# One row block at a time in the first stage, both column halves of a token tile in turn in the last MLP chunk, and a rearranged list of delays

## The chip, the cores and the metric

The kernel runs on one core of a Trainium2 chip. The metric is the device time of one execution in microseconds (us). The engines are named as in the profile: PE is the matrix engine (PEld its weight loads), DVE the vector engine, ACT the scalar engine, POOL the GpSimd engine, SP the engine that issues nearly all DMA here.

## What is computed

One inference step of a two-layer backbone over 640 tokens (128 context and 512 latent) of width 1024. Per layer:

```python
h = x * (1 + sc_a) + sh_a                      # modulation from silu(c) @ w_ada + b_ada
mq, mk, mv, mo, mg, sq, sk, sv, nq, nk, nv = split(h @ w_in + b_in)
mix = concat(mlstm(mq, mk, mv, mo, mg), window_attention(sq, sk, sv), neighbourhood_attention(nq, nk, nv))
x = layer_norm(ALPHA * x + g_a * (mix @ w_out), ln1_g, ln1_b)
f = square(relu((x * (1 + sc_m) + sh_m) @ w_mlp1)) @ w_mlp2        # 1024 -> 4096 -> 1024
x = layer_norm(ALPHA * x + g_m * f, ln2_g, ln2_b)
```

## The kernel before

All products are fp32 carried by three products of split operands: every weight and activation is kept as a rounded high part and the rest, and `hi*hi + lo*hi + hi*lo` is summed in PSUM. `piece` (L366 on) loads 512 columns of a weight into one of four raw buffers (`wraw`), copies the high part on ACT (L371) and subtracts on DVE (L372) into one of eight split buffers (`wsp`).

Tokens are five tiles of 128. `gemm_feat` (product at L477, tile name gfeat) gives feature-major results in two halves of 320 tokens, 24 products for a block of 128 features and a half. `gemm_tok` (product at L393, tile gtok) gives token-major results, 512 columns for a tile, three products for each of K row blocks. PSUM tiles of both come from the pool `gp` with three buffers; `sp` (one buffer of two halves), `op` and `tp` serve the attention steps.

**Order.** PE's instructions stand in the order in which the program emits them; the other engines' order and the allocation of buffers are set by a list scheduler with the program order as priority, and SP's DMA issues with them. Attention, mLSTM, modulation and transposes (`to_feat`, named f0 to f4 after the first LayerNorm and g0 to g4 after the second) are generators in a queue. A planner keeps a planned time `self.T`; between products `pump` takes the steps whose due time has passed. The table `LATER` adds tenths of a microsecond to the due time of a named step (layer, name: {step: delay}).

**Start** (`start`, L292 on). The first modulation is computed in four parts q. Part q loads weights (adaw, 2 MB each) and the transposed inputs (xTv), runs 64 small products (L244), transposes them (L266) and then writes row blocks q and q+4 of the modulated input Xt (L328 to L330; the low part of q+4 on POOL). `first` is a `gemm_feat` of three blocks over row blocks in four groups (i, i+4), 36 products each. PE's order is part 0, part 1, group 0, part 2, group 1, part 3, groups 2 and 3. Its six weight pieces go through the four raw buffers.

**MLP** (`mlp`). The 32 blocks of the hidden layer go in five chunks. Chunk 0 has six blocks by `gemm_feat` (four in one call, then one each). Each block is copied from PSUM into a value tile of two buffers (ACT, L1454), squared with relu on DVE (L1356), rounded on ACT (L1357), and the rest is subtracted on POOL (L1358). After block 1 come the sums of the transformed activations (`t_sums`, four DVE operations of 1280 columns) and the splits 1 and 2 (`t_split`), after block 3 the first half of the LayerNorm's gain and bias on the residual (`ln_half`: two rows in raw buffers, ten DVE operations at L1268 and L1269), after block 5 the second half. Later chunks form their blocks in pairs with fewer products (gpair, L1348). Each chunk then runs `gemm_tok` over all five token tiles for the column half q = 0, then for q = 1; after it the evacuation `ev` adds to the residual (L1198 to L1203) and, in the last chunk, collects statistics (L1205). After q = 1 of the last chunk a tile is normalized (L1512 and L1254, L1255 in layer 1) and in layer 0 handed to `to_feat` for the next layer. Where `between` is given, `gemm_tok` runs all but two row blocks of the first tiles ahead; in chunk 0 it isn't given.

## Time and profile before

| | |
|---|---|
| median of 3 runs | 1726.15 us (1725.24 to 1726.2) |
| profiled execution | 1726.68 us, span 1724.8 us |
| PE busy | 1620.9 us, 94% |
| PEld busy | 1403.1 us, 81% |
| DVE busy | 1177.1 us, 68% |
| ACT busy | 716.8 us, 42% |
| mean granted clock of PE | 0.972 |
| chain that ended last | PE 75%, DVE 11%, ACT 5%, DMA 4%, issue 3% |

The span is the time from the first to the last instruction. The profile counts a matmul from its start to a modelled end, so neighbouring matmuls overlap; PEclk is the share of full clock that was granted (1.00 is 2.4 GHz, half of it 1.2 GHz). In a list of instructions a number in brackets is the time the engine sat idle before, and what ended it; x24 means that 24 instructions of the kind were merged into one row.

### The profile page before, as it was taken

What the parts mean: (1) busy time and instruction counts of PE and PEld (TensorE: products, weight loads), DVE (VectorE), ACT (ScalarE), POOL (GpSimd) and SP (SyncE); (2) the same over time, 40 slices, a digit from 0 to 9 for tenths busy, and PEclk for the clock granted to TensorE, in tenths of its full rate; (3) what the DMA queues carried; (4) which work ended last, traced back from release to release, by engine and by line L of the source; (5) the groups of instructions that cost most, each with busy time, mean ns of one, the idle gap of its engine ahead of it and who ended that gap; (6) DMA issues with size and microseconds to landing.
All of it is one profiled execution on the core that took longest, in us unless ns stands there. A gap on an engine that the chain in (4) does not pass through costs nothing.

```text
span 1724.8 us, 27638 instructions
## 1 busy us (share of the span) xinstructions
PE 1620.9 (94%) x10396; PEld 1403.1 (81%) x10396; DVE 1177.1 (68%) x2477; ACT 716.8 (42%) x1640; POOL 214.7 (12%) x204
## 2 busy tenths in 40 slices
PE   5999799999999999999999998999998999999996
PEld 3988687778968787879888886888788898898985
DVE  3368767659857575757685778675797667676768
ACT  2342466655414142424353424666464243332430
POOL 0151000000301010112200510000002021111210
PEclk9999899999999999999999997999999999999998
DMA  8554434332235454542324331222322132322222
GB/s 308 199 167 130 133 124 138 117 98 80 83 125 189 135 184 140 180 145 74 108 92 139 101 97 53 67 65 79 105 86 86 50 98 73 95 69 83 74 78 81
DMA packets 105857, 195.23 MB, mean 113 GB/s; under 512 B 16474, under 2 KB 43098, under 8 KB 100604
## 3 DMA queue, kind: packets, MB, share of 16 engines
q1 hardware_dynamic: 105724, 193.47, 35.0%
q8 instruction: 82, 1.34, 0.3%
q14 instruction: 51, 0.42, 0.1%
HBM read 185.16 MB, written 8.26 MB: 112 GB/s over the span
## 4 chain that ended last, share of the span: by engine, by line
PE 75%; DVE 11%; ACT 5%; DMA 4%; issue 3%; POOL 1%; SPq 1%; DVEq 0%; ACTq 0%; POOLq 0%
PE gtok L393 35%; PE gpair L1348 19%; PE gfeat L477 10%; PE adaps L244 2%; PE o L1058 2%; PE ptp L1042 2%; ACT P L1013 2%; PE s L999 1%; DVE nm L1006 1%; DVE wst L372 1%; DVE P L1020 1%; PE mli L819 1%; DMA adab<-in_b_ada 1%; DMA nbias<-in_nbias 1%; ACT PT L1050 1%
## 5 line engine op out<-in xcount | busy, mean ns | idle before, releaser
L393 PE MATMUL gtok<-wst,f1T 128*128 128x512 f32 x1920 | 461.0, 398 | 5.9 <-ACT f1T L1357 3.1
L393 PEld LDWEIGHTS gtok<-wst,f1T 128*128 128x128 f32 x1920 | 361.7, 190 | 97.3 <-issue 5.9
L477 PE MATMUL gfeat<-Xt,wst 128*128 128x320 f32 x1920 | 316.0, 320 | 11.9 <-ACT f L1454 4.9
L477 PEld LDWEIGHTS gfeat<-Xt,wst 128*128 128x128 f32 x1920 | 292.8, 194 | 23.9 <-ACT f L1454 6.0
L371 ACT CAST wst<-wrawt 128x512 fp32r<-128x512 f32 (+2 forms) x288 | 167.5, 599 | 277.4 <-PE gtok L393 214.4
L1358 POOL TENSOR_TENSOR f1T<-f,f1T 128x320 fp32r<-128x320 f32 (+1 forms) x116 | 130.3, 1125 | 932.3 <-ACT f1T L1357 822.2
L372 DVE TENSOR_TENSOR wst<-wrawt,wst 128x512 fp32r<-128x512 f32 (+2 forms) x288 | 197.9, 701 | 69.4 <-ACT wst L371 67.6
L1348 PE MATMUL gpair<-Xt,wst 128*128 128x320 f32 x1248 | 195.1, 309 | 0.0
L1348 PEld LDWEIGHTS gpair<-Xt,wst 128*128 128x128 f32 x1248 | 186.2, 188 | 6.2 <-issue 2.5
L1198 DVE TENSOR_TENSOR gtok<-gtok,row 128x512 f32<-128x512 f32 x110 | 76.7, 697 | 163.5 <-PE gtok L393 162.8
L1316 ACT CAST wst<-wrawt 128x512 fp32r<-128x512 f32 x156 | 94.5, 620 | 196.3 <-DVE gtok L1198 106.5
L1317 DVE TENSOR_TENSOR wst<-wrawt,wst 128x512 fp32r<-128x512 f32 x156 | 112.5, 733 | 34.2 <-ACT wst L1316 34.0
L393 PE MATMUL gtok<-wst,Xt 128*128 128x384 f32 (+1 forms) x720 | 125.1, 329 | 7.1 <-DVE wst L372 7.1
L393 PEld LDWEIGHTS gtok<-wst,Xt 128*128 128x128 f32 x720 | 115.6, 192 | 11.0 <-DVE wst L372 8.3
L393 PE MATMUL gtok<-wst,yT 128*128 128x512 f32 x480 | 117.9, 399 | 1.6 <-DVE wov L1198 1.6
L393 PEld LDWEIGHTS gtok<-wst,yT 128*128 128x128 f32 x480 | 88.2, 188 | 23.1 <-DVE wov L1198 2.4
L1348 PE MATMUL gpair<-tq,wst 128*128 128x320 f32 x624 | 100.9, 310 | 0.0
L1348 PEld LDWEIGHTS gpair<-tq,wst 128*128 128x128 f32 x624 | 93.8, 188 | 4.8 <-issue 4.2
L1013 ACT ACTIVATE P<-P,nm 128x512 f32<-128x512 f32 (+2 forms) x120 | 80.6, 673 | 32.8 <-DVE nm L1008 15.0
L1357 ACT CAST f1T<-f 128x320 fp32r<-128x320 f32 (+1 forms) x116 | 56.4, 488 | 76.1 <-DVE f L1356 75.5
L1356 DVE SCALAR_TENSOR_TENSOR f<-f 128x320 f32<-128x320 f32 (+1 forms) x116 | 68.6, 593 | 26.2 <-ACT f L1427 19.3
L1006 DVE TENSOR_REDUCE nm<-P 128x2 f32<-128x1024 f32 (+2 forms) x60 | 66.5, 1108 | 15.6 <-ACT P L1095 8.7
(245 smaller groups left out, 1910.7 us busy)
## 6 DMA issues: line engine op xcount, KB each, us to landing
wrawt<-in_w SPq DMA_DIRECT2D x256, 256.0 KB
adaw<-in_w_ada SPq DMA_DIRECT2D x40, 1024.0 KB
wrawt<-in_w_f SPq DMA_DIRECT2D x56, 256.0 KB
adaw<-in_w_ada SPq DMA_DIRECT2D x16, 512.0 KB
wrawt<-in_w_o SPq DMA_DIRECT2D x32, 256.0 KB
Dt<-md SPq DMA_DIRECT2D x40, 128.0 KB
nbias<-in_nbias SPq DMA_DIRECT2D x18, 256.0 KB
wrawt<-in_w_tb SPq DMA_DIRECT2D x16, 192.0 KB
```

Source lines behind the costliest of these rows:

```text
L371: nc.scalar.copy(ws[:, 0, :], raw)
L372: nc.vector.tensor_tensor(out=ws[:, 1, :], in0=raw, in1=ws[:, 0, :].bitcast(F32), op=ALU.subtract)
L393: nc.tensor.matmul(o, lhsT=A[YORDER[k] if A is self.Y else k][:, hl, t * 128 : (t + 1) * 128], rhs=ws[k][:, wl, :], start=(k == 0 and hl + ...
L477: nc.tensor.matmul(g[i, h], lhsT=w[i][k // 4][:, wl, (k % 4) * 128 : (k % 4 + 1) * 128], rhs=self.Xt[:, k, hl, h * 320 : (h + 1) * 320], s ...
L1006: nc.vector.tensor_reduce(out=nm[:, 0:2], in_=P[:, :, 0:nk], axis=AX.X, op=ALU.max, negate=True)
L1013: nc.scalar.activation(P[:, h, 0:nk], P[:, h, 0:nk], AF.Exp, bias=nm[:, h : h + 1], accum_out=nm[:, 2 + h : 3 + h])
L1198: nc.vector.tensor_tensor(out=v, in0=o, in1=gr, op=ALU.mult)
L1316: nc.scalar.copy(w[name][:, 0, :], src)
L1317: nc.vector.tensor_tensor(out=w[name][:, 1, :], in0=src, in1=w[name][:, 0, :].bitcast(F32), op=ALU.subtract)
L1348: nc.tensor.matmul(o, lhsT=w[:, wl, k * 128 : (k + 1) * 128], rhs=rhs(k, hl), start=(start and k + hl + wl == 0), stop=(k == 3 and wl == 1 ...
L1356: nc.vector.scalar_tensor_tensor(out=f, in0=f, scalar=0.0, in1=f, op0=ALU.max, op1=ALU.mult)
L1358: nc.gpsimd.tensor_tensor(out=y[:, 1], in0=f, in1=y[:, 0].bitcast(F32), op=ALU.subtract)
```

## The change

Three things. At the start, `first` goes over single row blocks (0, 4, 1, 5, 2, 6, 3, 7), 18 products each; PE's order becomes part 0, block 0, part 1, block 4, part 2, blocks 1 and 5, part 3, the rest; the third weight's two raw pieces lie in the pool `tmp`. In chunk 0 of the MLP one block of a call takes its two PSUM halves from `sp` (`spread`); split 2 follows block 2 and split 1 block 3, each in two halves; the first LayerNorm half comes after all six blocks, and the second half's two rows are kept in raw buffers while its operations run tile by tile in the evacuation of q = 0 (`ln_tile`); the first two token tiles run four row blocks ahead. In the last chunk `gemm_both` takes both column halves of a tile before the next tile; the second half's weights are put into buffers that are free by then (Xt in layer 1; `p`, `tmp` and `aw` buffers in layer 0). The last LayerNorm of layer 1 is done in halves for all tiles, as it was for the last one. `LATER` changes in most entries.

```diff
     "0f2": {0: 10},
-    "0fin4": {0: 28},
-    "0g4": {0: 55, 1: -10},
-    "0ga": {0: 5},
+    "0fin0": {0: -10},
+    "0fin2": {0: 5},
+    "0g0": {0: 12},
+    "0g3": {0: 42},
+    "0g4": {0: 148},
+    "0ga": {0: 4, 1: 4},
...
-    "0ml4": {1: 11},
+    "0ml4": {1: 167},
...
-    "0s03": {0: 38},
+    "0s03": {0: 119},
...
-    "1s03": {0: 52, 3: 30},
+    "1s03": {0: 83, 3: 30},
...
         for q in range(4):
+            for _ in range((0, 1, 1, 2)[q]):
+                next(first)
             if q == 0:
-                first = self.gemm_feat(*[I["w_f"][0, m] for m in ML_FIRST[0][0]], kgroups=[(i, i + 4) for i in range(4)])
+                first = self.gemm_feat(*[I["w_f"][0, m] for m in ML_FIRST[0][0]], kgroups=[(k,) for k in (0, 4, 1, 5, 2, 6, 3, 7)])
                 next(first)
                 load(1)
...
-            if q > 0:
-                next(first)
-            if q == 3:
-                nc.sync.dma_start(self.cst, I["cst"])
+        for _ in range(3):
+            next(first)
+        nc.sync.dma_start(self.cst, I["cst"])
...
+    def gemm_both(self, A, src, evac, between):
...
+        if self.l == L - 1:
+            place = [x[:, :, 0:512] for x in self.X]
+        else:
+            place = [self.pp.tile([128, 2, 512], F32R, tag="p", name="wst") for _ in range(4)]
+            place += [self.tmp.tile([128, 2, 512], F32R, tag="tmp", name="wst") for _ in range(2)]
+            aw = self.adp.tile([128, 2, 2, 512], F32R, tag="aw", name="wst")
+            place += [aw[:, 0], aw[:, 1]]
+        ws = [[self.piece(b, 512) for b in src[0]], None]
+        later = lambda: ws.__setitem__(1, [self.piece(b, 512, w) for b, w in zip(src[1], place)])
...
+        early = {}
+        for t in range(2):
+            early[t] = self.gp.tile([128, 512], F32, tag="g", name="gtok")
+            for k in range(K - 2):
+                mm(early[t], 0, t, k)
+                if k % 2 == 1:
+                    self.q(self.six(512))
+                if (t, k) == (0, 1):
+                    between()
+                    later()
+        for t in range(NT):
+            for q in range(2):
+                o = early[t] if q == 0 and t in early else self.gp.tile([128, 512], F32, tag="g", name="gtok")
+                for k in range(K - 2 if q == 0 and t in early else 0, K):
+                    mm(o, q, t, k)
...
+                evac[q](t, o)
+                self.pump()
...
-        w = [self.feat_pieces(src) for src in srcs]
+        w = [self.feat_pieces(src) for src in srcs[: 2 if len(kgroups) > 1 else None]]
+        if len(kgroups) > 1:
+            w.append(self.feat_pieces(srcs[2], lambda: self.tmp.tile([128, 512], F32, tag="tmp", name="wrawt")))
...
-                    if (i, h) not in g and i == 2 and len(kgroups) > 1:
+                    if (i, h) not in g and i == (2 if len(kgroups) > 1 else spread):
                         s = self.sp.tile([128, 2, 512], F32, tag="s", name="gfeat")
...
-            nc.scalar.copy(hi, self.t32[w])
-            nc.vector.tensor_tensor(out=lo, in0=self.t32[w], in1=hi.bitcast(F32), op=ALU.subtract)
+            for k in (slice(0, 2), slice(2, 4)):
+                nc.scalar.copy(hi[:, k], self.t32[w][:, k])
+                nc.vector.tensor_tensor(out=lo[:, k], in0=self.t32[w][:, k], in1=hi[:, k].bitcast(F32), op=ALU.subtract)
...
-                rest = (g for j in range(4, 6) for g in self.gemm_feat(I["w1"][l, j]))
-                for j, g in enumerate(itertools.chain(self.gemm_feat(*first), rest)):
+                rest = (g for j in range(4, 6) for g in self.gemm_feat(I["w1"][l, j], spread=4 - j))
+                for j, g in enumerate(itertools.chain(self.gemm_feat(*first, spread=1), rest)):
...
                     if j == 1:
                         self.t_sums()
-                        self.t_split(1, 2)
-                    if j in (3, 5):
-                        self.ln_half(l, 0, j // 2 - 1)
+                    elif j in (2, 3):
+                        self.t_split(4 - j)
+                self.ln_half(l, 0, 0)
+                lnr = self.ln_rows(l, 0, 1)
                 self.t_split(3, 4)
...
                     self.ln_add(r, q, o, gr[int(t == 0)][q], ALPHA if c == 0 else 1.0, st.get(t))
+                    if c == 0 and q == 0:
+                        self.ln_tile(t, 1, lnr)
...
-                    if last and t == NT - 1:
+                    if last:
                         for h in range(2):
...
-                        self.add(self.to_feat(r, t, A, B), "feat", f + (0.5 if t < 3 else 5.0), f"g{t}")
...
+                    self.add(self.to_feat(r, t, A, B), "feat", self.use("V", 2.5, f) + 0.5, f"g{t}")
...
+            if c == NC - 1:
+                self.gemm_both(ft, [[I["w2"][l, q, j] for j in blocks] for q in range(2)], [ev(q) for q in range(2)], left)
+                break
...
-                self.gemm_tok(ft, [I["w2"][l, q, j] for j in blocks], 512, ev(q), between=left if q == 0 else None, ahead=2 if c < 4 else 3, inter=gen if q else None)
+                self.gemm_tok(ft, [I["w2"][l, q, j] for j in blocks], 512, ev(q), between=(left or (lambda: None)) if q == 0 else None, inter=gen if q else None)
```

## Rows read from the trace of the kernel before

**Rows 1.** The page, part 1: busy us, share of the span, instructions.

```profile
PE 1620.9 (94%) x10396; PEld 1403.1 (81%) x10396; DVE 1177.1 (68%) x2477; ACT 716.8 (42%) x1640; POOL 214.7 (12%) x204
```

**Rows 2.** Busy time by stage: us, PE, PEld, DVE, ACT, POOL, clock, DMA.

```profile
18.68:30.26 11.58, 4.45 (x65) 2.51 (x66) 4.27 (x8) 2.32 (x5) 1.53 (x1) 1.00 0.83 288
...
124.00:375.00 251.00, 228.27 (x1833) 189.75 (x1832) 171.36 (x451) 130.21 (x343) 16.74 (x17) 0.95 0.39 124
...
441.18:488.04 46.86, 40.85 (x215) 37.16 (x218) 33.35 (x41) 17.72 (x30) 14.87 (x6) 0.85 0.30 90
488.04:905.26 417.22, 417.10 (x2319) 350.49 (x2318) 278.48 (x488) 147.32 (x299) 52.17 (x55) 1.00 0.42 139
905.26:923.73 18.47, 14.02 (x83) 13.46 (x83) 14.25 (x29) 8.15 (x20) 0.00 (x0) 0.82 0.57 180
...
1000.00:1225.00 225.00, 204.26 (x1623) 176.51 (x1622) 154.56 (x401) 124.13 (x328) 10.83 (x9) 0.93 0.24 73
...
1290.17:1340.22 50.05, 45.36 (x243) 41.25 (x244) 35.98 (x40) 19.31 (x32) 11.42 (x6) 0.90 0.24 76
...
1711.11:1724.80 13.69, 0.00 (x0) 0.00 (x0) 10.35 (x25) 0.00 (x0) 0.00 (x0) 0.60 0.29 115
```

**Rows 3.** Timeline, the start: start us, us, engine, line, operation [idle before].

```profile
19.00 0.93 SPq L369 DMA_DIRECT2D wrawt<-in_w_f  x2
...
26.13 1.08 PE L244 MATMUL adaps<-adaw,cs 128*32 128x128 f32 x16 [6.37 <-DMA adaw<-in_w_ada]
...
30.26 7.41 PE L477 MATMUL gfeat<-Xt,wst 128*128 128x320 f32 x36
...
34.43 1.57 POOL L330 TENSOR_TENSOR Xt<-xTv,Xt 128x640 fp32r<-128x640 f32 x1 [11.71 <-DVE xTv L329]
...
40.05 5.53 PE L477 MATMUL gfeat<-Xt,wst 128*128 128x320 f32 x36
```

**Rows 4.** Timeline, first MLP chunk of layer 0 (its PE rows with PE alone).

```profile
441.70 3.78 PE L477 MATMUL gfeat<-Xt,wst 128*128 128x320 f32 x24 [0.52 <-ACT f L1454]
448.32 24.07 PE L477 MATMUL gfeat<-Xt,wst 128*128 128x320 f32 x144 [2.85 <-ACT f L1454]
...
479.00 9.04 PE L393 MATMUL gtok<-wst,f1T 128*128 128x512 f32 x26 [1.35 <-POOL f1T L1358]
...
443.45 4.36 POOL L1358 TENSOR_TENSOR f1T<-f,f1T 128x640 fp32r<-128x640 f32 x1 [150.73 <-ACT f1T L1357]
...
451.45 1.78 POOL L1358 TENSOR_TENSOR f1T<-f,f1T 128x640 fp32r<-128x640 f32 x1 [3.64 <-ACT f1T L1357]
...
456.85 23.00 SPq L369 DMA_DIRECT2D wrawt<-in_w  x12
...
465.67 1.28 DVE L1269 TENSOR_TENSOR res<-res,lnrow 128x512 f32<-128x512 f32 x2
```

**Rows 5.** Timeline of PE, first MLP chunk of layer 1.

```profile
1295.86 3.78 PE L477 MATMUL gfeat<-Xt,wst 128*128 128x320 f32 x24 [0.52 <-ACT f L1454]
1300.70 21.38 PE L477 MATMUL gfeat<-Xt,wst 128*128 128x320 f32 x144 [1.06 <-ACT f L1454]
...
1329.18 11.04 PE L393 MATMUL gtok<-wst,f1T 128*128 128x512 f32 x35 [1.34 <-POOL f1T L1358]
```

**Rows 6.** Timeline of PE, seam between the layers.

```profile
888.05 5.79 PE L393 MATMUL gtok<-wst,f1T 128*128 128x512 f32 x24
...
907.29 1.06 PE L531 MATMUL pth<-ident,res 128*128 128x128 f32 x8 [2.03 <-DVE res L1512]
...
911.41 12.32 PE L477 MATMUL gfeat<-Xt,wst 128*128 128x320 f32 x71 [0.41 <-DVE Xt L539]
```

**Rows 7.** Timeline, last chunk and tail of layer 1.

```profile
1656.70 54.41 PE L393 MATMUL gtok<-wst,f1T 128*128 128x512 f32 x234
...
1712.14 0.69 DVE L1198 TENSOR_TENSOR gtok<-gtok,row 128x512 f32<-128x512 f32 x1
...
1717.70 1.22 DVE L1255 TENSOR_TENSOR res<-res,row 128x1024 f32<-128x1024 f32 x1
```

More of the change, by code (lines that the diff above doesn't have):

```diff
@@ L431, in gemm_tok @@
         if between is not None:
-            for t in range(ahead):
+            for t in range(2):
                 early[t] = self.gp.tile([128, 512], F32, tag="g", name="gtok")[:, 0:n]
@@ L452, in gemm_tok, with mm @@
             self.pump()
-    def feat_pieces(self, src):
-        return [self.piece(src[:, j * 512 : (j + 1) * 512], 512) for j in range(2)]
-    def gemm_feat(self, *srcs, kgroups=(range(8),)):
+    def gemm_both(self, A, src, evac, between):
         nc = self.nc
-        w = [self.feat_pieces(src) for src in srcs]
+        K = len(A)
+        if self.l == L - 1:
[7 more added lines that the diff above has]
+        later = lambda: ws.__setitem__(1, [self.piece(b, 512, w) for b, w in zip(src[1], place)])
+        def mm(o, q, t, k):
+            for hl, wl in ((0, 0), (1, 0), (0, 1)):
+                nc.tensor.matmul(
+                    o, lhsT=A[k][:, hl, t * 128 : (t + 1) * 128], rhs=ws[q][k][:, wl, :],
+                    start=(k == 0 and hl + wl == 0), stop=(k == K - 1 and wl == 1),
+                )
+        early = {}
+        for t in range(2):
+            early[t] = self.gp.tile([128, 512], F32, tag="g", name="gtok")
[11 more added lines that the diff above has]
+                    mm(o, q, t, k)
+                    if k % 2 == 1 and k < K - 1:
+                        self.q(self.six(512))
+                self.T += self.six(512)
+                evac[q](t, o)
+                self.pump()
@@ L461, in gemm_feat, with feat_pieces @@
+    def feat_pieces(self, src, raw=lambda: None):
+        return [self.piece(src[:, j * 512 : (j + 1) * 512], 512, raw=raw()) for j in range(2)]
+    def gemm_feat(self, *srcs, kgroups=(range(8),), spread=None):
+        nc = self.nc
+        w = [self.feat_pieces(src) for src in srcs[: 2 if len(kgroups) > 1 else None]]
+        if len(kgroups) > 1:
+            w.append(self.feat_pieces(srcs[2], lambda: self.tmp.tile([128, 512], F32, tag="tmp", name="wrawt")))
         g = {}
@@ L481, in gemm_feat @@
                             )
-                        if n % 2 == 1 and (ks is not kgroups[-1] or (h, n) != (1, len(ks) - 1)):
+                        if len(ks) == 1:
+                            self.T += self.six(160)
+                        elif n % 2 == 1 and (ks is not kgroups[-1] or (h, n) != (1, len(ks) - 1)):
                             self.q(self.six(320))
@@ L1250, in tail1, with ln_rows @@
             self.gemm_tok(self.Y, I["w_o"][l, q], 512, ev(q), by_block=q == 0)
-    def ln_out(self, r, lg, lb, dst):
-        nc = self.nc
-        nc.vector.tensor_tensor(out=r, in0=r, in1=lg, op=ALU.mult)
-        nc.vector.tensor_tensor(out=r, in0=r, in1=lb, op=ALU.add)
-        if dst is not None:
-            nc.sync.dma_start(dst, r)
-    def ln_half(self, l, i, h, dst=None):
-        nc, I = self.nc, self.I
-        hs = slice(h * 512, (h + 1) * 512)
+    def ln_half(self, l, i, h, dst=None):
+        row = self.ln_rows(l, i, h)
+        for t in range(NT):
+            self.ln_tile(t, h, row, dst)
+        self.use("V", 6.8)
+    def ln_rows(self, l, i, h):
         row = []
```

118 lines of the change are left out of this document (67 added, 51 removed).

## The prediction

> **What bounds the kernel now.** I read the head of the page first: TensorE is busy for 1620.9 of 1724.8 us [rows 1]. What is not matmul time is the only thing a reordering can win, so the next view is busy time and granted clock by stage, and in it only the stages where PE is not full or the clock is under 1.00 [rows 2]. The long middle, 488 to 905 us, has 0.12 us of idle PE in 417 us at clock 1.00 [rows 2]: whatever runs beside the matmuls there is free. The losses sit in five other places: the start, the first MLP chunk of each layer, the seam between the layers, the two attention stretches, and the tail. Two rates turn stages into losses: 144 products of 320 columns took 21.38 us, 148.5 ns each [rows 5], and 234 products of 512 columns took 54.41 us, 232.5 ns each [rows 7]; both at full clock. A stage's loss is its length less its products at these rates, so it holds the idle time and the time run at half clock after it. In the first chunk of layer 0 the clock reads 0.85 [rows 2], although idle is only 6 us of 47: a wait there costs about twice its length.
>
> **The start.** PE waits for weights of the modulation until 26.13, 6.37 us idle, and only after that runs the first 36 products, in 7.41 us where the next 36 took 5.53 [rows 3]. The change cuts each group of 36 into two of 18 and puts the first 18 ahead of the second modulation block. They need row block 0 only, which the first modulation block has produced, and the last two pieces of weights. These are issued as late as 19.00 [rows 3] because there are four raw buffers; the change gives them two of their own, and the modulation loads queued behind them on SP move up too. The stretch 18.68 to 30.26 has 11.58 - 4.45 = 7.1 us of idle PE [rows 2]; 18 products even at half clock (2 x 18 x 0.1485 = 5.3) fit in it. Gain if only they vanish from the path: 18 x 0.1485 = 2.7. If the loads behind also land so much earlier that no idle time is left: 7.1. If the 18 push the second modulation block later by 0.4: 2.3. The next late thing is row block 5, whose low half leaves POOL at 34.43 + 1.57 = 36.0 [rows 3]; it is needed behind two more steps of PE, so it stays hidden. I take **-3.5**, ends -7.1 and -2.3, nearer to the low end since the modulation loads stay bound by DMA, whose share in that stretch is already 0.83 [rows 2].
>
> **First MLP chunk, the six blocks.** In layer 0 the products stop 2.85 us at 448.32, for a copy that waits until POOL has released the first value tile; POOL's subtraction took 4.36 us there and 1.78 us the next time [rows 4]. From 441.70 - 0.52 = 441.18 to 448.32 + 24.07 = 472.39 PE did 7 x 24 products: 31.2 - 24.9 = 6.3 us lost. In layer 1, from 1295.86 - 0.52 = 1295.34 to 1300.70 + 21.38 = 1322.08 [rows 5]: 26.7 - 24.9 = 1.8. The change gives one block of each call two more PSUM halves, moves ten LayerNorm operations on DVE behind the blocks and halves the splits. The sixth group of products then needs no copy, but the seventh still waits for the first value tile: from 441.18 to 448.32 that took 7.1 us, with POOL at 1.78 instead of 4.36 it takes 4.6, and one group of 24 (3.6 us) covers it. So 1 us of wait stays, 2 if POOL is held up in part, and the clock may or may not hold. I take **-3.5** and **-1**; ends -6.3 and 0, -1.8 and 0.
>
> **First MLP chunk, the start of the second product.** From 472.39 to 479.00 + 9.04 = 488.04 PE did 15 + 1 + 26 = 42 products [rows 4]: 15.65 - 9.77 = 5.9 lost, waiting for the last block's POOL result. In layer 1, 1322.08 to 1340.22 with 51 products [rows 5]: 18.14 - 11.86 = 6.3. The change lets the second token tile's first four blocks go ahead: 12 products, 2.8 us more cover, which is as much as the wait itself. What is late next is weights. The rows of the second LayerNorm half now hold two of the four raw buffers through the whole pass, and the first half's hold the other two until its ten operations are done. Before, twelve pieces took 23.00 us to issue, 1.9 us each, and the LayerNorm half that ran beside them ended at 465.67 + 1.28 = 466.9 [rows 4]. Six pieces need 11.5 us; PE needs the last one 27 x 0.2325 = 6.3 us after it begins at about 468. They are on time if the LayerNorm half ends by about 462, and 5 us late if at 466.9. I take half, **-3** in each layer; ends -6 and 0. The LayerNorm operations that move into the evacuation cost nothing beside the matmuls: four operations of 0.69 are 2.8 us per tile, against 18 x 0.2325 = 4.2 us of products; without that cover they would cost 1.4 us a tile.
>
> **Seam between the layers.** Before, DVE has evacuation, statistics, normalization and the split of a tile inside 5.8 us of products [rows 6] and falls behind. The last gtok product ends at 888.05 + 5.79 = 893.84; the transposes of the last tile start at 907.29 after 2.03 us of waiting, and the products run again at full pace only from 911.41. From 905.26 to 923.73: 18.47 us for the transposes (1.06) and 72 products (10.7), 6.7 lost, clock 0.82 [rows 2]. With both halves of a tile in turn there are 11.2 us of products per tile, so the last tile finds DVE free: three operations of 0.69 [rows 7], statistics and normalization (an estimated 3 us) end some 5 us after the last product rather than 13. The 2.03 us wait goes. But the new delay list puts this tile's transposes 14.8 us late, so they still stand directly ahead of products that need their result, and the second wait (2 us) stays. **-3.5**, ends -6.7 and 0.
>
> **Tail.** 13.69 us with no product [rows 2]. The last tile's evacuation starts at 1712.14, 1.03 after the last product at 1711.11, and the previous tile's operations lie between its own: two of 1.22 [rows 7], one of them shown, and five shorter that I estimate at 0.9 to 1.2. With the tile order changed these are done before the last product ends: -1.03 - 2.44 - 0.9 = **-4.4**, ends -4.9 and -3. What follows the last operation, the output transfer, stays.
>
> **The new second half of the weights** of the last chunk is loaded while the first is used, into buffers that are otherwise dead by then. It is needed 42 x 0.2325 + 24 x 0.1485 = 13.3 us after the pass begins. Eight pieces at 1.9 us, the rate of [rows 4], would take 15.2: nothing, up to +2 in each layer.
>
> **The delay list.** It reorders side steps of the attention stretches on PE. Those stretches lose 22.7 us idle and 0.05 x 251 at half clock in layer 0, 20.7 and 0.07 x 225 in layer 1 [rows 2], some 72 us together. No row shows which steps change places; by the nearest ones a wait as at 448.32, with its half clock, is 6.3 us. I take 0, with ends of -8 and +8.
>
> **Sum.** -3.5 - 3.5 - 1 - 3 - 3 - 3.5 - 4.4 = -21.9. The profiled execution took 1726.7 us (span 1724.8 and 1.9 around it), 0.5 over the median of the runs, 1726.15. 1726.15 - 21.9 = **1704**. All good ends together give 1687 before the list, all bad ones 1721, or 1725 with the late second half.
>
> **Rivals.** *Raw buffers (A).* The LayerNorm rows keep the weights of the second product waiting: the two -3 go, and half of the -3.5 of layer 0 with the half clock that follows; the late second half costs 2. Then -22 + 6 + 1.7 + 2 = -12: 1714. For it: the transfers stood 23 us at this place already. Against: loads of the fifth and sixth block no longer stand behind LayerNorm rows.
> *POOL locked out (B).* POOL's 4.36 us came while DVE did subtractions and multiplications of two SBUF operands, its 1.78 us when DVE ran little beside it [rows 4]. The ten LayerNorm operations now come behind the six blocks, where PE waits for the last block's subtraction on POOL: 2.6 us more there in each layer eat the 2.8 us of new cover, and the two -3 go, but not the rest: 1726 - 16 = 1710.
> The Trainium skill (SBUF - State Buffer, Who interferes with whom) has the rule for it: a DVE instruction with two SBUF inputs and a GpSimd instruction that reads SBUF exclude each other for the whole instruction, and the first to issue wins. The 4.36 us agree with it; by that rule the move would not pay.
> *Slower (C).* The list puts one side step per attention block ahead of its data, in a PE queue that can't pass it; every product behind it waits and then runs at half clock, 6.3 us a time as at 448.32. Four such places beyond today's (25 us) decide it; six of them give 1704 + 38 = 1742. For it: 72 us are lost there already in this way. Against: most of the list's changes are under 1 us of planned time.
> *No change (D).* The gains are given back at the next wait on a chain that doesn't move. Against: nothing in these stages is tied to a fixed time, and PE is full from 488 to 905 [rows 2], so a shift is handed on. 1726.
>
> **How the numbers follow.** Forecast 0.57, A 0.18, B 0.10, C 0.10, D 0.05. The range: the forecast's own ends with the list's give 1690 to 1714, and A's late side reaches 1720; below 1690 and above 1720 (C, D) I leave about 0.2. So 1690 to 1720. A measurement of this kernel tells 0.2%, 3.5 us, from no change: faster holds forecast, A and B, 0.85; D 0.05; slower C, 0.10.
>
> **What would show it.** Right: 18 products of gfeat before 26 us; the wait at 448 under 2 us and the first-chunk stages above 0.95 clock; 27 products without a break at the start of gtok; the last tile's transposes not waiting for the normalization; under 10 us after the last product. Wrong: waits of PE on wst at the start of gtok (A), POOL over 3 us on the last block (B), the two attention stretches more than 10 us longer (C).

## The result, and the profile after

The changed kernel takes **1703.2 us** (median of 4 runs, 1699.7 to 1712.0) against 1726.2 beside it: a ratio of 0.987, 95% interval 0.983 to 0.991. The forecast was 1704, its range 1690 to 1720. The profiled execution has a span of 1699.4 us, 25.4 less than before, and TensorE is busy for 7.2 us less in it [rows 1]. First the head of the page, then busy time by stage, cut at the places that answer to those of [rows 2] (us, PE, PEld, DVE, ACT, POOL, clock, DMA share, GB/s):

```profile
PE 1613.7 (95%) x10396; PEld 1394.4 (82%) x10396; DVE 1188.2 (70%) x2489; ACT 715.3 (42%) x1648; POOL 213.8 (13%) x204
```

```profile
14.60:26.62 12.02, 8.04 (x84) 6.39 (x84) 6.72 (x16) 5.39 (x10) 2.47 (x1) 1.00 0.98 357
117.54:368.54 251.00, 233.90 (x1883) 192.60 (x1881) 176.46 (x460) 133.14 (x350) 17.44 (x17) 0.95 0.40 129
429.03:471.68 42.65, 38.48 (x218) 34.18 (x220) 40.25 (x50) 18.23 (x34) 15.46 (x6) 0.92 0.33 99
471.68:888.89 417.21, 417.08 (x2319) 350.71 (x2318) 284.42 (x496) 146.82 (x299) 51.89 (x55) 1.00 0.43 141
888.89:905.48 16.59, 13.53 (x81) 13.09 (x81) 8.86 (x20) 8.30 (x20) 0.00 (x0) 0.90 0.52 160
981.91:1206.91 225.00, 201.63 (x1635) 174.97 (x1636) 154.81 (x415) 123.64 (x329) 11.02 (x10) 0.95 0.25 75
1267.43:1316.28 48.85, 44.31 (x251) 39.38 (x250) 46.61 (x55) 24.14 (x47) 11.11 (x6) 0.93 0.26 81
1689.46:1699.40 9.94, 0.00 (x1) 0.00 (x0) 6.37 (x17) 0.00 (x0) 0.00 (x0) 0.68 0.14 53
```

The middle (471.68 to 888.89) is as full as before. To see where 25.4 us went, I cut the kernel at the first product of each kind in TensorE's timeline. Lengths in us, from one profiled execution each; "again" is a second profile of the changed kernel, from another session:

| stretch | before | after | again | after - before |
|---|---|---|---|---|
| start, to the first token projection | 58.60 | 52.14 | 53.25 | -6.5 |
| layer 0, projections and attention | 362.85 | 357.65 | 360.77 | -5.2 |
| layer 0, six blocks of the first chunk | 50.77 | 44.19 | 44.18 | -6.6 |
| layer 0, their second product | 49.54 | 51.38 | 51.54 | +1.8 |
| layer 0, the other chunks | 371.92 | 372.72 | 372.72 | +0.8 |
| seam, to layer 1's first token projection | 29.89 | 27.40 | 27.39 | -2.5 |
| layer 1, projections and attention | 346.69 | 347.41 | 349.23 | +0.7 |
| layer 1, six blocks | 51.66 | 46.44 | 46.46 | -5.2 |
| layer 1, their second product | 45.20 | 45.95 | 46.68 | +0.7 |
| layer 1, the other chunks | 343.99 | 344.18 | 344.15 | +0.2 |
| tail, after the last product | 13.69 | 9.94 | 9.93 | -3.8 |

The 0.8 us that layer 0's other chunks are longer go with one token tile's transposes: that stretch holds 2088 TensorE instructions where it held 2080, and eight transposes of a tile take 1.03 us.

The timelines behind the rows that moved. The start, TensorE and SP's queue (start, length, what; the gap before in brackets), to be held against [rows 3]:

```profile
9.51 5.49 SPq L389 DMA_DIRECT2D wrawt<-in_w_f  x6
...
17.58 0.90 PE L543 MATMUL gfeat<-Xt,wst 128*128 128x320 f32 x2 [2.98 <-ACT wst L392]
...
24.17 1.95 PE L262 MATMUL adaps<-adaw,cs 128*32 128x128 f32 x64
```

All six weight pieces are issued in one go, 18 products run in the stretch that was idle, and the second modulation block finds its weights there at 24.17, where it waited until 26.13 and was fed in pieces before.

The first chunk, layer 0 and then layer 1, against [rows 4, 5]:

```profile
420.45 33.68 PE L543 MATMUL gfeat<-Xt,wst 128*128 128x320 f32 x228
...
457.12 3.50 PE L414 MATMUL gtok<-wst,f1T 128*128 128x512 f32 x14 [0.24 <-DVE wst L393]
461.80 0.73 PE L414 MATMUL gtok<-wst,f1T 128*128 128x512 f32 x2 [1.18 <-POOL f1T L1428]
463.84 0.52 PE L414 MATMUL gtok<-wst,f1T 128*128 128x512 f32 x1 [1.31 <-ACT f1T L1427]
465.80 4.63 PE L414 MATMUL gtok<-wst,f1T 128*128 128x512 f32 x10 [1.44 <-POOL f1T L1428]
...
431.90 1.94 POOL L1428 TENSOR_TENSOR f1T<-f,f1T 128x640 fp32r<-128x640 f32 x1 [154.49 <-ACT f1T L1427]
...
455.50 6.25 POOL L1428 TENSOR_TENSOR f1T<-f,f1T 128x640 fp32r<-128x640 f32 x1 [6.61 <-ACT f1T L1427]
...
462.22 0.81 DVE L1426 SCALAR_TENSOR_TENSOR f<-f 128x640 f32<-128x640 f32 x1
...
1269.70 0.42 PE L543 MATMUL gfeat<-Xt,wst 128*128 128x320 f32 x1 [0.26 <-ACT Xt L606]
1270.97 28.52 PE L543 MATMUL gfeat<-Xt,wst 128*128 128x320 f32 x191 [0.86 <-DVE Xt L607]
...
1301.15 0.50 PE L414 MATMUL gtok<-wst,f1T 128*128 128x512 f32 x1 [0.48 <-DVE wst L393]
1302.61 0.73 PE L414 MATMUL gtok<-wst,f1T 128*128 128x512 f32 x2 [0.95 <-ACT wst L392]
1304.91 1.65 PE L414 MATMUL gtok<-wst,f1T 128*128 128x512 f32 x3 [1.57 <-DVE wst L393]
1306.98 18.26 PE L414 MATMUL gtok<-wst,f1T 128*128 128x512 f32 x70 [0.42 <-DVE wst L393]
```

In layer 0 the six blocks now run without a break; in layer 1 two short waits for the last token tile's Xt are left, 0.26 and 0.86 us. The second product starts worse than before. In layer 0 it waits 1.18 us for GpSimd's subtraction of the fifth block, which takes 6.25 us, and then 1.31 and 1.44 us for the sixth block, whose square comes only at 462.22, 8.2 us after the second product has begun. In layer 1 it waits for weights, 3.4 us in four waits. Before, layer 1's waits for Xt were longer, and 23 products behind the second took 5.17 us:

```profile
1287.96 0.41 PE L477 MATMUL gfeat<-Xt,wst 128*128 128x320 f32 x1 [1.14 <-ACT Xt L538]
1290.17 5.17 PE L477 MATMUL gfeat<-Xt,wst 128*128 128x320 f32 x23 [1.80 <-DVE Xt L539]
```

The seam, TensorE and then VectorE with the last tile's normalization (L1279 to L1585), against [rows 6]:

```profile
878.08 10.81 PE L543 MATMUL gfeat<-Xt,wst 128*128 128x320 f32 x72
889.31 1.07 PE L599 MATMUL pth<-ident,res 128*128 128x128 f32 x8 [0.43 <-DVE res L1585]
892.39 0.41 PE L543 MATMUL gfeat<-Xt,wst 128*128 128x320 f32 x1 [2.01 <-ACT Xt L606]
893.43 12.21 PE L543 MATMUL gfeat<-Xt,wst 128*128 128x320 f32 x71 [0.63 <-DVE Xt L607]
...
881.43 0.20 DVE L1279 BATCH_NORM_AGGREGATE bmv<-bst 128x2 f32<-128x12 f32 x1
881.54 0.77 DVE L1339 TENSOR_TENSOR res<-res,lnrow 128x512 f32<-128x512 f32 x1
...
888.37 0.80 DVE L1585 TENSOR_SCALAR res<-res,bmv 128x1024 f32<-128x1024 f32 x1
```

The tail, against [rows 7]: the last evacuation starts with nothing of the previous tile between its steps.

```profile
1683.74 5.72 PE L492 MATMUL gtok<-Xt,f1T 128*128 128x512 f32 x24
...
1689.50 0.70 DVE L1266 TENSOR_TENSOR gtok<-gtok,row 128x512 f32<-128x512 f32 x1 [2.31 <-PE gtok L492]
...
1694.84 1.41 DVE L1582 SCALAR_TENSOR_TENSOR res<-res,bmv,row 128x512 f32<-128x512 f32 x2
```

### The profile page after: what moved, and what is told of

Same layout as the page of the kernel before. It is cut to its first block, busy times and chain, and to the rows that moved or that the text cites. A ratio compares the mean times of both kernels' runs of the same rounds, so it can differ in the third digit from the quotient of the medians.

```text
span 1699.4 us, 27642 instructions
## 1 busy us (share of the span) xinstructions
PE 1613.7 (95%) x10396; PEld 1394.4 (82%) x10396; DVE 1188.2 (70%) x2489; ACT 715.3 (42%) x1648; POOL 213.8 (13%) x204
## 4 chain that ended last, share of the span: by engine, by line
PE 75%; DVE 11%; DMA 4%; issue 4%; ACT 4%; SPq 1%; POOL 1%; DVEq 0%; POOLq 0%; ACTq 0%
PE gtok L414 31%; PE gpair L1418 19%; PE gfeat L543 8%; PE gtok L492 6%; PE ptp L1110 2%; PE o L1126 2%; PE adaps L262 2%; PE s L1067 2%; ACT P L1081 1%; PE mli L887 1%; DMA adaw<-in_w_ada 1%; DVE res L1338 1%; DVE wst L393 1%; DMA nbias<-in_nbias 1%; DVE res L1339 1%
## 5 line engine op out<-in xcount | busy, mean ns | idle before, releaser
L414 PE MATMUL gtok<-wst,f1T 128*128 128x512 f32 x1440 | 349.4, 400 | 7.7 <-DVE wst L393 2.7
L414 PEld LDWEIGHTS gtok<-wst,f1T 128*128 128x128 f32 x1440 | 271.1, 190 | 80.4 <-issue 5.9
L543 PE MATMUL gfeat<-Xt,wst 128*128 128x320 f32 x1920 | 309.5, 317 | 10.2 <-ACT wst L392 4.9
L543 PEld LDWEIGHTS gfeat<-Xt,wst 128*128 128x128 f32 x1920 | 286.8, 191 | 22.5 <-ACT wst L392 6.1
L392 ACT CAST wst<-wrawt 128x512 fp32r<-128x512 f32 (+2 forms) x280 | 162.4, 597 | 224.7 <-PE gtok L414 157.4
L492 PE MATMUL gtok<-wst,f1T 128*128 128x512 f32 x360 | 85.5, 395 | 0.0
```

What stands on the lines that cost most here:

```text
L392: nc.scalar.copy(ws[:, 0, :], raw)
L414: nc.tensor.matmul(o, lhsT=A[YORDER[k] if A is self.Y else k][:, hl, t * 128 : (t + 1) * 128], rhs=ws[k][:, wl, :], start=(k == 0 and hl + ...
L492: nc.tensor.matmul(o, lhsT=A[k][:, hl, t * 128 : (t + 1) * 128], rhs=ws[q][k][:, wl, :], start=(k == 0 and hl + wl == 0), stop=(k == K - 1 ...
L543: nc.tensor.matmul(g[i, h], lhsT=w[i][k // 4][:, wl, (k % 4) * 128 : (k % 4 + 1) * 128], rhs=self.Xt[:, k, hl, h * 320 : (h + 1) * 320], s ...
```

## The experiments

All start from the changed kernel. Stretch lengths are cut as in the table above, each from the one profile of its run.

**The same kernel again.** No edit.

> The changed kernel once more, nothing edited. Its four runs lie between 1699.7 and 1712.0 us where the kernel before kept within 5 us. Theory 1: the spread sits in the stages whose waits the change left or made (the start of the second product in the first MLP chunk, 7.8 and 6.9 us lost in the profile at hand, and the attention stretches), so a second profile shows the start (to 52.3 us), the six blocks (33.7 us for 228 products) and the tail (9.9 us) within 0.3 us, and those stages different by several us. Theory 2: the whole is slower by a common factor, then the dense middle (chunks 1 to 3) is longer too. Time 1700 to 1712 by both.

1705.5 us (1702.7 to 1709.0), ratio 0.988 (0.986 to 0.990). The dense stretches repeat to 0.1 us; the start, the attention and layer 1's second product don't. So a small difference of a stage is read only in the stretches that repeat: eleven profiles with one and the same order in layer 0's attention have it at 357.4 to 362.9 us, and before, at 362.85, lies inside. The start, in the eleven profiles that have both of its edits, lies between 51.75 and 54.06.

**The start, in two halves.** In start_raw the third weight goes back into the four raw buffers:

```diff
-        w = [self.feat_pieces(src) for src in srcs[: 2 if len(kgroups) > 1 else None]]
-        if len(kgroups) > 1:
-            w.append(self.feat_pieces(srcs[2], lambda: self.tmp.tile([128, 512], F32, tag="tmp", name="wrawt")))
+        w = [self.feat_pieces(src) for src in srcs]
```

> Undoes one third of the change at the start: the third weight's two raw pieces go back into the four shared raw buffers, so the second modulation block's loads again stand in SP's queue behind a piece that waits for a free buffer; the order of the products stays one row block at a time. The first product of the first token projection starts at 58.60 us in the kernel before and at 52.14 in the changed one. Theory (both parts count, the queue 3.6 us and the 18 products in idle time 2.9 us): 55.0 to 56.5. If the whole gain is the queue: 58 to 59. If the whole gain is the product order: 52 to 53. The rest of the kernel is that of the changed one.

In start_grp the buffers stay and the order goes back:

```diff
-            for _ in range((0, 1, 1, 2)[q]):
-                next(first)
...
-                first = self.gemm_feat(*[I["w_f"][0, m] for m in ML_FIRST[0][0]], kgroups=[(k,) for k in (0, 4, 1, 5, 2, 6, 3, 7)])
+                first = self.gemm_feat(*[I["w_f"][0, m] for m in ML_FIRST[0][0]], kgroups=[(i, i + 4) for i in range(4)])
...
-        for _ in range(3):
-            next(first)
+            if q > 0:
+                next(first)
```

> The other half of the start: the third weight's raw pieces keep their own buffers, but the products are grouped in pairs of row blocks and taken after each modulation block, as in the kernel before. Theory (both parts count): first product of the first token projection at 54.5 to 56.0, the second modulation block's last TensorE product ends near 26 us as in the changed kernel instead of 29.7. If the whole gain is the queue: 52 to 53. If the whole gain is the product order: 58 to 59.

The first token projection starts at 54.90 in start_raw and 54.00 in start_grp, between 52.14 and 58.60 and a little earlier than I expected. By these profiles the order alone is worth 3.7 us, the free queue alone 4.6, both 6.5: each half alone brings more than half of the gain. What the second half adds to the first is not shown: 54.00 lies inside the 51.75 to 54.06 of the profiles with both edits, and 54.90 only 0.8 us outside. start_raw took 1703.9 us as a whole, in one run. Its timeline shows the piece that holds the queue at 18.71 and the modulation block behind it:

```profile
18.71 0.93 SPq L389 DMA_DIRECT2D wrawt<-in_w_f  x2
...
25.98 1.85 PE L262 MATMUL adaps<-adaw,cs 128*32 128x128 f32 x48
28.23 0.64 PE L262 MATMUL adaps<-adaw,cs 128*32 128x128 f32 x16 [0.40 <-DMA adaw<-in_w_ada]
```

start_grp as a whole took 1718.8 us in its one run, 13 to 16 above the changed kernel's two medians: layer 0's attention is 369.7 us long there, outside the 357.4 to 362.9 of the others, with one wait of 5.87 us where the longest in those is 3.2. My explanation, that the planner's clock moves with the grouping and the list of delays no longer fits, was not tested.

**Six blocks: the extra PSUM halves, or the LayerNorm's place?** no_spread takes the halves away:

```diff
-                rest = (g for j in range(4, 6) for g in self.gemm_feat(I["w1"][l, j], spread=4 - j))
-                for j, g in enumerate(itertools.chain(self.gemm_feat(*first, spread=1), rest)):
+                rest = (g for j in range(4, 6) for g in self.gemm_feat(I["w1"][l, j]))
+                for j, g in enumerate(itertools.chain(self.gemm_feat(*first), rest)):
```

> Undoes one part in the first MLP chunk alone: no block of the six gets the two extra PSUM halves; the layer-norm operations and the halved splits stay as in the changed kernel. The six blocks with what precedes them take 44.2 us in layer 0 and 46.4 in layer 1 in the changed kernel, without a wait of TensorE. Theory (the extra PSUM halves are what covers the copy of the first block): a wait for the copy comes back ahead of the sixth and seventh group of products, 47 to 51 us in layer 0 and 48 to 52 in layer 1. Rival (VectorE's order and the halved splits make the copy early enough): 44 to 45 and 46 to 47.

ln_old writes the first LayerNorm half, its two rows in raw buffers included, back among the blocks:

```diff
-                self.ln_half(l, 0, 0)
+                    if j == 3:
+                        self.ln_half(l, 0, 0)
                 lnr = self.ln_rows(l, 0, 1)
```

> The other part: the ten layer-norm operations of the first half are written back among the six blocks (behind the fourth), the extra PSUM halves stay. In the changed kernel's trace VectorE runs the first of these operations at 432.78, already between the squares of the first and second block, although they are written behind all six; so the place where they are written should matter little. Theory: 44.0 to 45.0 us and 46.0 to 47.0 us for the six blocks, as in the changed kernel, and the second product's start within 2 us of its 51.4 and 46.0 to 46.7. Rival (moving them behind the blocks is what freed GpSimd): the first block's subtraction takes over 3 us instead of 1.94, and the stretch is 2 to 4 us longer.

In no_spread the six blocks take 45.78 us in layer 0 and 48.12 in layer 1, 1.6 and 1.7 more than with the halves: in layer 0 between my theory and the rival, in layer 1 at the low end of the theory. Two waits of 0.5 to 0.65 us for the copy came back in each layer; in layer 0:

```profile
432.44 3.78 PE L543 MATMUL gfeat<-Xt,wst 128*128 128x320 f32 x24 [0.52 <-ACT f L1524]
436.76 21.39 PE L543 MATMUL gfeat<-Xt,wst 128*128 128x320 f32 x144 [0.55 <-ACT f L1524]
```

The second product takes 50.31 and 46.48 us behind them, so of blocks and product together 0.5 us is left in layer 0 and 2.2 in layer 1. The one run took 1705.6 us, like the changed kernel.

In ln_old the six blocks take 46.56 and 49.30, 2.4 and 2.8 more. My theory (the written place matters little) falls. In layer 0 the rival holds: GpSimd's first subtraction takes 6.37 us while VectorE runs LayerNorm beside it, and the copy behind it keeps TensorE waiting. In layer 1 it is VectorE's own order: the last tile's split into Xt stands behind LayerNorm operations, and TensorE waits 2.41 us for it instead of 0.86.

```profile
438.35 6.37 POOL L1428 TENSOR_TENSOR f1T<-f,f1T 128x640 fp32r<-128x640 f32 x1 [156.18 <-ACT f1T L1427]
...
445.22 17.86 PE L543 MATMUL gfeat<-Xt,wst 128*128 128x320 f32 x120 [2.12 <-ACT f L1524]
...
1283.33 29.81 PE L543 MATMUL gfeat<-Xt,wst 128*128 128x320 f32 x191 [2.41 <-DVE Xt L607]
```

But the second product then starts better: 49.54 and 40.71 us instead of 51.4 and 46.0. Blocks and product together are 96.10 and 90.01 with the old place, 95.57 and 92.39 with the new one. So moving the LayerNorm half behind the blocks mostly moved the loss: the sum gained 0.5 us in layer 0 and lost 2.4 in layer 1. The one run of ln_old took 1709.6 us, with layer 1's attention at 351.3, the longest of all profiles; its total says nothing of this edit.

**Second product: weights or GpSimd?** rows_late issues the LayerNorm's rows behind the six weight pieces, so that no row holds a raw buffer ahead of a weight; the ten operations that need the first two rows move with them:

```diff
-                self.ln_half(l, 0, 0)
-                lnr = self.ln_rows(l, 0, 1)
+                self.use("V", 6.8)
+                lnr = []
...
+                def left():
+                    self.ln_half(l, 0, 0, busy=False)
+                    lnr.extend(self.ln_rows(l, 0, 1))
```

> In the first MLP chunk the LayerNorm rows of both halves and the ten operations of the first half are put behind the six weight pieces of the second product, so the pieces take the raw buffers first; the order of PE and the planned times stay. Theory A (raw buffers held by the rows keep the weights waiting): the waits of PE on wst at the start of the second product (0.2 us in layer 0, 3.4 us in layer 1) vanish, the loss of that stage falls from 6.9 to under 3 us in layer 1. Theory B (LayerNorm operations on DVE shut POOL out): the subtraction of block 4 in layer 0, 6.25 us, falls to under 3, and the 3.9 us of waits on the last blocks' results fall below 2; the loss there falls from 7.8 to about 3. By both together the time falls by 6 to 9 us, 1694 to 1697; by A alone by 4, by B alone by 4. Rival: the ten operations now delay the first evacuation, the products stop for a PSUM buffer instead, and the time stays at 1703.

1709.1 us (1704.9 to 1711.1), no gain. TensorE's waits for weights are gone in both layers. In layer 0 the stretch is 49.4 us, 2.0 shorter; in layer 1 it is 49.0, 2.3 to 3.1 longer: now the last block is late there too.

```profile
1312.21 0.50 PE L414 MATMUL gtok<-wst,f1T 128*128 128x512 f32 x1 [2.09 <-ACT f1T L1428]
1318.26 12.06 PE L414 MATMUL gtok<-wst,f1T 128*128 128x512 f32 x43 [5.56 <-POOL f1T L1429]
...
1312.23 5.98 POOL L1429 TENSOR_TENSOR f1T<-f,f1T 128x640 fp32r<-128x640 f32 x1 [6.60 <-ACT f1T L1428]
```

In layer 0 the fifth block's subtraction is back at 1.80 us, yet the sixth block stays late, for a reason that I had not listed: ScalarE's copy of its second half out of PSUM stands in ScalarE's queue behind a weight cast that waits 4.56 us for a transfer.

```profile
464.46 0.62 ACT L392 CAST wst<-wrawt 128x512 fp32r<-128x512 f32 x1 [4.56 <-DMA wrawt<-in_w]
464.98 0.42 ACT L1525 COPY f<-gfeat 128x320 f32<-128x320 f32 x1
```

That copy starts 6.2 us after the second product has begun, and in layer 0 of the changed kernel just as late (6.2); in ln_after and ln_pool below it starts 0.2 us after. So late weights also reach TensorE through ScalarE's copy, without a wait of TensorE for weights. No run takes this apart.

So several causes stand one behind the other, and taking one away hands the stall to the next. ln_after, on top of seam_early (below), takes away all of them: rows in other buffers, the LayerNorm operations behind the sixth block, its subtraction on VectorE.

```diff
+                def left():
+                    for h in range(2):
+                        row = self.tmp.tile([128, 2, 512], F32, tag="tmp", name="lnrow")
...
+                    done = self.relu2(ft[j], f.rearrange("p h t -> p (h t)"), sub=nc.vector if j == 5 else None)
...
+                    if c == 0 and q == 0:
+                        with self.tc.issue_after(done.ins):
+                            self.ln_tile(t, 0, lnr[0])
```

> seam_early, and in the first MLP chunk of both layers: the layer-norm rows go into the two buffers that the sums of the activations leave (no raw weight buffer is held), all twenty layer-norm operations are queued on VectorE behind the sixth block's last step, and that step, the sixth block's subtraction, goes on VectorE instead of GpSimd. Reading of the runs so far: at the start of the second product TensorE waits for the raw buffers (weights, layer 1), for GpSimd's subtraction held up beside VectorE's layer-norm operations (both layers), and for the square of the last block, which stands behind layer-norm operations on VectorE. All three go here. The stretch from the first product with the squares to the first pair product takes 51.4 us (layer 0) and 46.0 to 46.7 (layer 1) in the changed kernel; theory: 44.5 to 48 and 40 to 43, the whole kernel 6 to 11 us below seam_early, 1688 to 1694. Rival (the layer-norm operations, now between the evacuations, make the second column half's weights late): the same stretches 50 to 53 and 45 to 48 with a wait on the weights at the start of the second half, the total within 3 us of seam_early's 1699.3.

ln_pool is ln_after with the sixth block's subtraction on GpSimd again, and the LayerNorm queued behind that block's square:

> ln_after with the sixth block's subtraction left on GpSimd; the twenty layer-norm operations stand on VectorE directly behind the sixth block's square, so they run while GpSimd subtracts. If operations on VectorE that read two inputs from SBUF hold up GpSimd, the sixth block's subtraction takes 5 to 6.5 us instead of 1.8, TensorE waits 3 to 5 us for it in each layer, and the kernel is 5 to 10 us slower than ln_after. If only the order on VectorE counts (the square behind the layer norm), it takes 1.8 to 2.1 us and the kernel is within 3 us of ln_after.

ln_after takes **1685.4 us** (1683.0 to 1691.3), ratio 0.976 (0.974 to 0.979); ln_pool 1686.8 (1680.3 to 1689.0), the same ratio; both are better than I expected of ln_after. The second product is 43.6 and 44.6 us in layer 0 and 39.0 in layer 1 for both, 7 to 8 us less than in seam_early and dense in layer 1:

```profile
1296.46 39.19 PE L414 MATMUL gtok<-wst,f1T 128*128 128x512 f32 x168
```

GpSimd's subtraction took 1.79 and 1.81 us in ln_pool, although LayerNorm operations run from its start on; here it was a VectorE operation beside it that took 2.06 instead of 0.68 us.

```profile
461.42 1.79 POOL L1429 TENSOR_TENSOR f1T<-f,f1T 128x640 fp32r<-128x640 f32 x1 [5.09 <-ACT f1T L1428]
...
460.49 1.29 DVE L1339 TENSOR_TENSOR res<-res,lnrow 128x512 f32<-128x512 f32 x2
461.69 2.06 DVE L1340 TENSOR_TENSOR res<-res,lnrow 128x512 f32<-128x512 f32 x1
```

So the first of the two expectations for ln_pool falls and the second holds: the engine of that subtraction is not what costs the 7 us. What does is the order on VectorE or the held buffers, with ScalarE's copy behind them; both runs change these together, and their shares are not shown.

**The seam.** seam_early puts the last LayerNorm's operations behind layer 1's first token projection and lets the last tile's transposes go early; seam_ln does the first alone (it keeps the delay of 148):

```diff
-                self.ln_half(l - 1, 2, m // 2, self.xd)
+                self.use("V", 6.8)
...
+            for h in range(2):
+                self.ln_half(l - 1, 2, h, self.xd, busy=False)
...
-    "0g4": {0: 148},
+    "0g4": {0: 10},
```

> Gain and bias of the last LayerNorm of layer 0 on the residual (twenty DVE operations of 0.68 us) are put behind the next layer's first token-major projection, and the delay of the last tile's transposes is 1.0 us instead of 14.8. Theory: at the seam those operations stand between the short operations of the last tile's reciprocal root (881.4 to 889.2 us for what takes 3 us in the tail), and the transposes stand directly ahead of products that need them; without both, the normalization ends by 884, the transposes run inside the 72 products, the waits of 0.43, 2.01 and 0.63 us and the half clock behind them go: 4 to 5 us, 1698 to 1699. Rival 1: the transposes now come too early and PE waits for the normalization, 1 to 3 us: 1701 to 1704. Rival 2: the moved operations hold up the next stage (gates, output-gate buffer), and the gain is lost there: 1703.

> One of the two edits of seam_early alone: the twenty layer-norm operations of layer 0's last norm are put behind the first token projection of layer 1, and the last token tile's transposes stay where the changed kernel's delay list puts them (delay 148). Theory (both the interleaved operations and the place of the transposes count): the stage at the layer seam takes 24 to 26 us (27.4 in the changed kernel, 22.1 in seam_early); the last tile's chain of ten short operations on VectorE takes some 3 us instead of 7.7. If the operations on VectorE explain it all: 22 to 23. If the place explains it all: 27 to 27.6.

seam_early: 1699.3 us (1694.4 to 1706.7), ratio 0.985 (0.983 to 0.988), seam 22.07 us instead of 27.4; the range of its runs overlaps that of the changed kernel, so the gain is read from the seam. seam_ln: a seam of 26.48, just above what I expected, 1705.7 us in one run. The last tile's chain on VectorE, ten short operations and the normalization, is 3.6 us long in it instead of 7.7 (881.43 to 889.17 above), yet this is worth only 0.9 us; the place of the transposes is worth 4.4 with it. With the transposes behind 42 products instead of 72, their result is there when it is needed:

```profile
877.86 6.41 PE L543 MATMUL gfeat<-Xt,wst 128*128 128x320 f32 x42
884.11 1.04 PE L599 MATMUL pth<-ident,res 128*128 128x128 f32 x8
884.90 15.20 PE L543 MATMUL gfeat<-Xt,wst 128*128 128x320 f32 x102
```

**Both halves of a tile in turn.** no_both takes the last chunk in two passes again (`if c == NC - 1` becomes `if c == NC`):

> Undoes the last chunk's part alone: its second product goes in two passes over the five token tiles, one for each column half, as in the kernel before; everything else is the changed kernel. Theory: the time from the last TensorE product to the end goes back from 9.94 us to 13.5 to 14.0, and the stretch from the last pair products of layer 0 to the first weight product of layer 1 loses the little that it had gained (27.4 us to 28.5 to 31); the whole kernel 5 to 7 us above the changed one (about 1711, with a spread of 4 from run to run). Rival (taking both halves of a tile in turn costs in the chunk itself what it saves in the tail, by converting eight more pieces early): the last chunk of either layer gets 2 to 4 us shorter here and the total stays within 2 us of the changed kernel.

1707.2 us in two runs, ratio 0.988 (0.984 to 0.993), 2 to 4 us above the changed kernel's two medians, inside the spread of its runs, and not 5 to 7. The tail is 11.3 us, not 13.5 to 14; the seam 28.8, and layer 0's chunks 0.8 shorter. By the stretches, taking both halves in turn is worth 1.3 us in the tail and 0.6 at the seam, 1.9 in all. That leaves 2.4 of the tail for the other edit there, the last norm in halves for every tile, which was not run alone.

**The list of delays.** list_old is the changed kernel with the old table.

> The changed kernel with the delay list of the kernel before. My forecast put the list at 0 with ends of 8 us either way: 1695 to 1711. From the two profiles the attention stretch of layer 0 came out 5 us shorter with the new list and that of layer 1 0.7 longer, so by the profiles 1707 to 1709. Rival: the list carries more than half of the whole gain, since the planned times have moved and the old delays no longer fit: over 1715.

1715.1 us, ratio 0.993 (0.992 to 0.995), 9.6 above the changed kernel beside it: the rival holds. Layer 0's attention takes 366.9 us (357.4 to 362.9 with the new list), layer 0's other chunks 376.8 instead of 372.7, layer 1's six blocks 2.1 more. In the attention one wait of TensorE is 5.76 us, where the longest with the new list is 3.2; in the last chunk of layer 0 TensorE waits 1.07 and 2.20 us for the normalization of a tile that it is to transpose:

```profile
188.76 0.45 PE L1026 MATMUL ptko<-ident,kx 128*128 128x128 f32 x1 [5.76 <-DVE rsq L556]
...
885.57 1.07 PE L581 MATMUL pth<-ident,res 128*128 128x128 f32 x8 [2.20 <-DVE res L1567]
```

The new list on the kernel before was not run, so what the list is worth there is not known.

## Why the prediction was right, point by point

The total came out as forecast, -23.0 in the medians for -21.9. The stretches that the forecast priced also add up to it, -22 in the profile. But the terms missed on both sides, the list's among them, and that they cancelled so closely is luck. Of the five signs that I named for being right two came (18 products before 26 us, under 10 us after the last product) and one in part (no wait at 448, but a clock of 0.92 and 0.93 in the first chunks, not 0.95); the two others did not come: the second product's start breaks off in both layers, and the last tile's transposes wait 0.43 us for the normalization. Of the signs of being wrong, waits on wst came, and a subtraction over 3 us, of the fifth block. The range, too, was narrower than its own working: the ends add up to 1687 to 1721 before the list, not to 1690 to 1714 with it.

- **Start**, -3.5 forecast, -6.5 in this profile and -4.5 to -6.9 over the profiles with both edits: the mechanism was right, the size toward the good end. I held the gain low because the modulation loads were bound by DMA (share 0.83). The share rose to 0.98, and with the queue free the second block's loads came earlier: in part the queue, and not the transfer rate, had been the limit.
- **Six blocks**, -3.5 and -1, came out at -6.6 and -5.2. In layer 0 every wait went, also the 1 us that I left in, and the granted clock of the first chunk rose from 0.85 to 0.92. Each taken back alone, the PSUM halves are worth 1.6 and 1.7, the LayerNorm's place 2.4 and 2.8; if the two add up, 2.6 of layer 0 weren't taken apart. In layer 1 I counted the loss of the last seven groups of products alone (1.8). The five before them held more: the waits for the last tile's Xt were 1.14 and 1.80 us, with 23 products behind them in 5.17 us (3.4 at 148.5 ns each), and are 0.26 and 0.86 now. The old list brings 2.1 us of that back.
- **Start of the second product**, -3 in each layer: the step that failed, with the wrong sign, +1.8 and +0.7. I had weighed the raw buffers against the new cover and taken half. Both rivals were there at once, GpSimd's delay (B) in layer 0 and the raw buffers (A) in layer 1. Neither rival had the sixth block's late copy and square, which hold TensorE for 2.75 of the 4.2 us of waits in layer 0. rows_late shows that the next cause takes over when one goes. Part of the gain of the six blocks is this loss, put later.
- **Seam**, -3.5 forecast, -2.5: I let the first wait (2.03) go whole and kept the second. The first became 0.43, because nine LayerNorm operations stand between the last tile's ten short ones; the second stayed, for the reason given, the transposes' place. The part of the edit that I credited, both halves in turn, is worth 0.6.
- **Tail**, -4.4 forecast, -3.8, but the tile order, to which I credited all of it, brings 1.3; the other 2.4 are left for the norm in halves.
- **Late second half of the weights**, 0: right, no wait in the last chunk of either layer; 24 products in 5.72 us up to the end.
- **The list**, 0 with ends of 8: mis-sized. Against the kernel before, layer 0's attention stays within its spread, which looks like 0. But on the new code the list is worth 9.6 us, beyond the good end: with the old list the gain is 12.0 us, with the new one in the same session 21.6. So the other edits, which I had at -21.9, bring 12.0 without the list that goes with them. Two parts of the 9.6 are seen in list_old: the waits for a tile's normalization in the last chunk, 3.3 us, and the one long wait in the attention. That the other edits shift the planner's clock is my explanation of the second; it was not tested.

So the mechanisms of A and B came true, at some 9 us against the sum (-6 forecast, +2.6), and the start and the six blocks, which I had counted 10.3 us too low in this profile, happened to pay for them.

## What to carry to other kernels

When a wait is taken away, list everything that was late behind it: here weights, a copy, a square and a subtraction were late one behind the other, and only the two versions in which none of them was late any more (1685 and 1687 us) got the cover's worth. Work without a deadline, such as a LayerNorm that the next stage needs late, belongs behind the operations that an engine waits for, and where a scheduler orders a queue by its own estimate, that order has to be tied down. A table of delays tuned to one order is part of that order: change both, or measure both apart.

## What the runs showed of the hardware

GpSimd's subtraction of 128x640 mostly takes 1.5 to 2.1 us. It took 5.98 (rows_late), 6.25 (the changed kernel), 6.37 (ln_old) and 9.43 us (layer 0 of no_spread) where VectorE runs operations with two SBUF operands without a gap, most of them 0.68 to 0.82 us long; values between, such as 4.94 us in layer 0 of start_raw, occur too. In ln_old the subtraction, issued at 438.35, ends at 444.72, 1.4 us after VectorE's last such operation (443.3). So it stood for eight operations, seven of which start after it, and not for one. The Trainium skill (SBUF — State Buffer, Who interferes with whom) says that such a VectorE instruction and a GpSimd instruction that reads SBUF exclude each other for the whole instruction and that the first to issue wins. The traces agree with the exclusion: in ln_pool the VectorE operation beside a running subtraction takes 2.06 us instead of 0.68. That a queue of them can keep GpSimd out for many in a row is what these rows add. In ln_pool the same neighbours let it in after one, and no row shows what made the difference; that stays open.
